# A hybrid decoder block on one core: the gated blocks exchanged inside SBUF, the left-side sums of down begun a group sooner, and a fourth pair by seven products

## The chip, the cores and the metric

The kernel runs on one NeuronCore of a Trainium2 chip. The metric is device time in microseconds of one execution; lower is better. The engines are named as in the profile: PE is TensorE's matmuls and PEld its weight loads, DVE is VectorE, ACT is ScalarE, POOL is GpSimd, SP is the engine that here only issues DMAs. L12 is line 12 of the kernel's source.

## The reference

One layer of a decoder block on 256 tokens of width 2048, everything in float32. The change lies in the two feed-forward halves (FFN 1 and FFN 2):

```
def swiglu(x, w_gu, w_down):
    gate, up = jnp.split(x @ w_gu, 2, axis=-1)      # 2048 -> 2 x 5632
    return (jax.nn.silu(gate) * up) @ w_down        # 5632 -> 2048

h = h + 0.5 * swiglu(rms_norm(h, ffn1_norm), ffn1_w_gu, ffn1_w_down)
h = h + hybrid_mixer(rms_norm(h, mix_norm), ...)    # gated DeltaNet and stick-breaking heads
h = h + 0.5 * swiglu(rms_norm(h, ffn2_norm), ffn2_w_gu, ffn2_w_down)
h = h + sigmoid(rms_norm(h, ple_norm) @ ple_w_gate) * (p @ ple_w_proj)
return rms_norm(h, final_norm)
```

## The kernel before

**Float32 out of two halves.** Every float32 operand is split into a rounded high half and the rest (`whi` and `wlo` for weights, `hTh` and `hTl` for activations), and each product is three matmuls: high by high, low weight by high, high weight by low. A weight pair (256 rows by 512 columns) is loaded into `raw` (SP's queue, four buffers), cast to `whi` by ACT (L77) and reduced to `wlo` by DVE (L78), two pairs ahead of its use. It then feeds 12 matmuls of 128x128 by 512 columns.

**Groups.** An FFN runs in three parts of 3, 4 and 4 blocks of 512 hidden columns (`PARTS`). Each part has its gate/up groups ("gu", one for each block: banks g0, g1, u0, u1) and then two down groups ("dn", two output blocks of 512 each, all in banks named d). A group has some of its pairs by seven products instead of eight (Strassen's scheme over two token halves and two column halves), and the others plainly. The number by products is `NS` = 4 for gate/up; for down, `NS_DOWN` gives 2 in part 0 and 3 in parts 1 and 2.

**Products.** A product needs a weight sum and a left-side sum. The weight quarters `R` (1 MB for four pairs) come on POOL's queue; their sums are formed by DVE (L307) or by accumulating DMAs; each of the seven is cast to `shi` by ACT (L298) and reduced to `slo` by DVE (L299), two buffers each, and feeds 3 matmuls per pair (L342 to L344). The seven products of a group are computed in the middle of the group ahead of it, between that group's plain pairs. The left-side sums (`halves`, L423: `S`, then its halves `Sh` and `Sl`) are made from the activations' halves: `S` by DVE (L455, L461), `Sh` by ACT (L463), `Sl` by DVE (L464). For down they begin with the last gate/up group of a part (L525).

**From up to down.** When a gate/up group's gate is done, ACT applies Silu (`gated`, L508). When up is done, `down_input` (L473) multiplies (`sil`, L480), transposes in blocks of 32 by 32 (`tb`, L485), exchanges the blocks through DRAM (four writes `scr`, L491, then one read `tT`, L496) and splits the result into `hTh` (L502) and `hTl` (L503), which the plain down matmuls and the left-side sums read. The writes go out on ACT's queue, and on SP's for the last block of a part.

**What sets the order.** `plan` writes one list of weight pairs, sums and loads, which is followed as it stands. Side work lives in generators on `lanes` (lane 0: the exchange; lane 1: left-side sums): each plain pair advances every lane by one step, `finish` runs a lane out, and a `yield` is one step's delay. A scheduler then orders each engine's instructions by its own costs; `keep_in_program_order` pins one. Each DMA also takes one of eight semaphores in turn, and waits until the earlier transfer on that semaphore has landed.

Of the kernel before, what the change touches and what calls it, by code (L numbers as in the profile page):

```python
# [20 lines left out]
NB = 512  # L21
# [5 lines left out]
PARTS = ((0, 3), (3, 7), (7, 11))  # L27


NS = 4  # L30
NS_DOWN = tuple(3 if i1 - i0 == 4 else 2 for i0, i1 in PARTS)


SEVEN = (0, 1, 2, 4, 3, 5, 6)
# [12 lines left out]
def block_kernel(ctx, tc, a, out):  # L47
    nc = tc.nc
# [4 lines left out]
    act = ctx.enter_context(tc.tile_pool(name="act", bufs=1))  # L53
# [9 lines left out]
    lanes = Lanes(4)  # L63
    dr = ctx.enter_context(tc.tile_pool(name="dr", bufs=1, space=bass.MemoryType.DRAM))
# [358 lines left out]
    def halves(kind, his, los, ns, wait=0):  # L423


        for _ in range(wait):
            yield
        fp = current[0]

        sh = fp.tile([P, NS, 2, 2, P], F32R, tag="Sh", name="Sh")  # L430
        sl = fp.tile([P, NS, 2, 2, P], F32R, tag="Sl", name="Sl")

        def side(i, g):
            if i in (0, 4, 6):
                k, t = 2 * (g % 2) + (i > 0), i // 6
                c = slice(t * P, (t + 1) * P)
                return his[g // 2][:, k, c], los[g // 2][:, k, c]
            j, t = {1: (1, 1), 2: (0, 0), 3: (0, 1), 5: (1, 0)}[i]
            return sh[:, g, j, t, :], sl[:, g, j, t, :]

        sides[kind] = side

        for g0 in range(0, ns, 2):
            n = min(2, ns - g0)
            hi, lo = his[g0 // 2], los[g0 // 2]
            keep = lambda ins: ins
            if g0 and n == 1:

                keep = tc.keep_in_program_order
                yield  # L450
            if n == 2:
                x = fp.tile([P, 2 * NB], F32, tag="sil", name="S")
            else:
                x = act.tile([P, NB], F32, tag="nat", name="S", bufs=4)
            keep(nc.vector.tensor_tensor(out=x, in0=hi[:, 0:2 * n].bitcast(F32).rearrange("p k x -> p (k x)"),  # L455
                                         in1=lo[:, 0:2 * n].bitcast(F32).rearrange("p k x -> p (k x)"), op=ALU.add))
# [7 lines left out]
            nc.vector.tensor_tensor(out=sx[1], in0=x, in1=sx[0], op=ALU.subtract)  # L464
            yield

    def ffn(n, nT, r, scale, next_norm, stat):
        xs = picker(*nT)
        late = callable(r)
        with tc.tile_pool(name="ffn", bufs=1) as fp:  # L470
            hTh, hTl = [], []

            def down_input(u, sil, th, tl, last):  # L473

                queue, keep = (nc.sync, lambda x: x) if last else (nc.scalar, tc.keep_in_program_order)
                for t in range(2):
                    nc.vector.scalar_tensor_tensor(out=sil[:, t, :], in0=u[t], scalar=r[:, t:t + 1], in1=sil[:, t, :],  # L480
                                                   op0=ALU.mult, op1=ALU.mult)
                yield
                tb = fp.tile([P, 4, 2, P], F32, tag="tT", name="tb")
                for t in range(2):
                    nc.vector.transpose(tb[:, :, t].rearrange("p c (j x) -> p c j x", j=4),  # L485
                                        sil[:, t, :].rearrange("p (j c x) -> p c j x", j=4, c=4))
                if not last:
                    yield
                scr = dr.tile([P, 4, 2, P], F32, tag="scr2", name="scr2", bufs=2)
                for q in range(4):  # L490
                    keep(queue.dma_start(out=scr[:, q].rearrange("(c x) t i -> x c (t i)", c=4),  # L491
                                         in_=tb[32 * q:32 * q + 32].rearrange("x c t i -> x c (t i)")))
                for _ in range(2 if last else 4):
                    yield
                tT = fp.tile([P, 4, 2, P], F32, tag="tT", name="tT")
                keep(nc.sync.dma_start(out=tT, in_=scr))  # L496
                for _ in range(last or 6):
                    yield
                for t in range(2):
                    hi, lo = (x[:, :, t * P:(t + 1) * P].rearrange("p j (q y) -> p q j y", q=4) for x in (th, tl))  # L500
                    tv = tT[:, :, t].rearrange("p q (j y) -> p q j y", j=4)
                    keep(nc.scalar.copy(hi, tv))  # L502
# [8 lines left out]
            nxt = None  # L511
            current[0] = fp
            lanes.add(1, halves("gu", *nT, NS, 6 if late else 0))
            for group, todo in ffn_plan[n]:
                if group.kind == "behind":
                    break
                dn = group.kind == "dn"
                i0 = PARTS[group.part][0]

                if dn and group.nb and not group.last:  # L520
                    lanes.add(1, halves("gu", *nT, NS))
                elif dn and group.nb and group.follower:
                    lanes.add(1, halves("behind", *nxt, NS_BEHIND, 4))
                elif not dn and group.follower.kind == "dn":
                    lanes.add(1, halves("dn", hTh[i0:], hTl[i0:], NS_DOWN[group.part]))  # L525
                if dn and group.last and nxt is None:
                    nxt = new_nT()
                if group.banks is None:
                    group.new_banks()
                for kind, one in todo:  # L530
                    if kind == "seventh":
                        group.follower.product(SEVEN[one])
                        continue
                    b, g = one
                    whi, wlo = next_weights()
                    for j in range(2):
# [3 lines left out]
                        for t in range(2):  # L540
# [3 lines left out]
                            nc.tensor.matmul(out, xh[:, c], wlo[:, j, :], start=False, stop=False, skip_group_check=True)  # L544
                            nc.tensor.matmul(out, xl[:, c], whi[:, j, :], start=False, stop=sp, skip_group_check=True)  # L545
                    lanes.step()
                    if g < len(group.src[b]) - 1:
                        continue
                    outs = group.banks[2 * b:2 * b + 2]
                    if dn:  # L550
                        nb = group.nb + b
                        for t in range(2):
                            hb = h[:, t, block(nb)]
                            nc.vector.scalar_tensor_tensor(out=hb, in0=outs[t], scalar=scale, in1=hb,
                                                           op0=ALU.mult, op1=ALU.add)
                            if group.last:
                                sumsq(stat, t, block(nb), nb)
                        if group.last:
                            norm_block(nxt, next_norm, nb, lambda: fp.tile([P, 2, 4, P], F32, tag="tT", name="tT"),
                                       mm_ps if group.follower or n == "2" else mx_ps)  # L560
                            lanes.advance(0)
                    elif b == 0:
                        if not late:
                            sil = gated(outs)
                    else:
                        if late:
                            r = r()
                            sil = gated(group.banks[0:2])
                            late = False
# [12 lines left out]
                        if last:  # L582
                            lanes.advance(0)
# [797 lines left out]
```

## Time and profile before

| | |
|---|---|
| median of 3 runs | 1948.04 us (1947.73 to 1949.59) |
| profiled execution | 1948.68 us |
| its span | 1947.0 us |
| granted TensorE clock | 0.999 of full speed |
| PE busy | 1930.5 us, 99% |
| PEld busy | 1593.0 us, 82% |
| DVE busy | 1569.3 us, 81% |
| ACT busy | 1163.5 us, 60% |
| DMA | 475.04 MB, 244 GB/s on average |

The span runs from the first to the last instruction; the execution's own time has 1.68 us around it. Matmuls overlap, so that PE's busy share says little: what counts is how far apart the starts of matmuls lie, and where they lie further apart than in an undisturbed stream. A row of waits has the engine, the line, what it waited for, the total in us, the times and the longest. A row of a window has the stretch, then busy us and the number of instructions of PE, PEld, DVE, ACT and POOL, the clock, the DMA share and GB/s.

### The profile page before, as it was taken

How to read it: one execution, taken by the hardware profiler on the slowest of the kernel's cores; microseconds unless marked ns; L12 is line 12 of the kernel's file. 1: busy time of each engine (PE TensorE's matmuls, PEld its weight loads, DVE VectorE, ACT ScalarE, POOL GpSimd, SP SyncE). 2: the span in 40 equal slices, each digit the busy share in tenths (PEclk: the TensorE clock that was granted, in tenths of full speed). 3: DMA queues.
4: the chain of work that ended last, by engine and by line, in shares of the span. 5: the costliest groups of instructions: out<-in, count | busy, mean ns of one | idle time of the engine just before them, and what ended most of it. 6: DMA issues, size and time to landing. Idle time of an engine off the chain costs nothing.

```text
span 1947.0 us, 24130 instructions
## 1 busy us (share of the span) xinstructions
PE 1930.5 (99%) x8884; PEld 1593.0 (82%) x8884; DVE 1569.3 (81%) x1679; ACT 1163.5 (60%) x1358; POOL 148.4 (8%) x226
## 2 busy tenths in 40 slices
PE   9999999999999999999999999999999999999998
PEld 8888888888888888878788888888888888888886
DVE  7889878997889766797856579899888987888865
ACT  7656666566565557664555456566565755656654
POOL 0011100000010000010100000010000100001000
PEclk9999999999999999999999999999999999999999
DMA  8778888788887765556565786788898987888764
GB/s 314 267 238 282 254 296 273 229 294 250 279 284 240 225 219 170 176 171 208 171 204 160 242 290 227 225 291 283 243 281 249 314 260 240 272 255 293 232 213 144
DMA packets 144182, 475.04 MB, mean 244 GB/s; under 512 B 19649, under 2 KB 47297, under 8 KB 129857
## 3 DMA queue, kind: packets, MB, share of 16 engines
q1 hardware_dynamic: 107200, 302.16, 43.9%
q0 software_dynamic: 25920, 160.44, 30.2%
q10 hardware_dynamic: 10944, 10.91, 1.8%
q8 instruction: 69, 1.13, 0.2%
q14 instruction: 49, 0.39, 0.1%
HBM read 451.44 MB, written 22.02 MB: 243 GB/s over the span
## 4 chain that ended last, share of the span: by engine, by line
PE 88%; DVE 7%; DMA 3%; ACT 1%; issue 1%; POOL 0%; SPq 0%; POOLq 0%; DVEq 0%; ACTq 0%
PE d L545 5%; PE d L543 5%; PE d L544 5%; PE g L343 4%; PE g L344 4%; PE g L342 4%; PE u L544 4%; PE u L545 4%; PE u L543 4%; PE g L544 4%; PE g L545 4%; PE pj L112 4%; PE pj L113 4%; PE pj L114 4%; PE g L543 4%; PE d L343 2%
## 5 line engine op out<-in xcount | busy, mean ns | idle before, releaser
L77 ACT CAST whi<-raw 128x1024 fp32r<-128x1024 f32 (+1 forms) x489 | 512.1, 1050 | 422.7 <-PE pj L114 99.0
L78 DVE TENSOR_TENSOR wlo<-raw,whi 128x1024 fp32r<-128x1024 f32 (+1 forms) x489 | 592.3, 1218 | 162.3 <-ACT whi L77 161.2
L299 DVE TENSOR_TENSOR slo<-R,shi 128x2048 fp32r<-128x2048 f32 (+2 forms) x224 | 444.9, 1989 | 140.0 <-ACT shi L298 138.2
L298 ACT CAST shi<-R 128x2048 fp32r<-128x2048 f32 (+2 forms) x224 | 373.5, 1671 | 128.5 <-DVE R L307 62.7
L112 PE MATMUL pj<-whi,nTh 128*128 128x512 f32 x448 | 179.4, 401 | 0.0
L113 PE MATMUL pj<-wlo,nTh 128*128 128x512 f32 x448 | 175.2, 391 | 1.1 <-DVE wlo L78 1.1
L114 PE MATMUL pj<-whi,nTl 128*128 128x512 f32 x448 | 174.9, 390 | 0.0
L543 PE MATMUL d<-whi,hTh 128*128 128x512 f32 x448 | 174.5, 390 | 0.0
L544 PE MATMUL d<-wlo,hTh 128*128 128x512 f32 x448 | 174.3, 389 | 0.0
L545 PE MATMUL d<-whi,hTl 128*128 128x512 f32 x448 | 173.4, 389 | 0.0
L544 PE MATMUL g<-wlo,nTh 128*128 128x512 f32 x400 | 156.0, 390 | 0.5 <-DVE wlo L78 0.5
L544 PE MATMUL u<-wlo,nTh 128*128 128x512 f32 x400 | 155.7, 389 | 0.4 <-DVE wlo L78 0.4
L545 PE MATMUL g<-whi,nTl 128*128 128x512 f32 x400 | 155.8, 389 | 0.0
L545 PE MATMUL u<-whi,nTl 128*128 128x512 f32 x400 | 155.7, 389 | 0.0
L543 PE MATMUL g<-whi,nTh 128*128 128x512 f32 x400 | 155.3, 390 | 0.0
L543 PE MATMUL u<-whi,nTh 128*128 128x512 f32 x400 | 154.1, 389 | 0.0
L307 DVE TENSOR_TENSOR R<-R 128x2048 f32<-128x2048 f32 (+2 forms) x68 | 135.8, 1996 | 0.1
L113 PEld LDWEIGHTS pj<-wlo,nTh 128*128 128x128 f32 x448 | 84.2, 188 | 18.9 <-DVE wlo L78 2.6
L543 PEld LDWEIGHTS d<-whi,hTh 128*128 128x128 f32 x448 | 84.1, 188 | 18.2 <-ACT hTh L502 1.0
L545 PEld LDWEIGHTS d<-whi,hTl 128*128 128x128 f32 x448 | 84.1, 188 | 17.8
L114 PEld LDWEIGHTS pj<-whi,nTl 128*128 128x128 f32 x448 | 84.1, 188 | 17.5
L544 PEld LDWEIGHTS d<-wlo,hTh 128*128 128x128 f32 x448 | 84.1, 188 | 17.4
(332 smaller groups left out, 3444.1 us busy)
## 6 DMA issues: line engine op xcount, KB each, us to landing
raw<-in_w_gu SPq DMA_DIRECT2D x199, 512.0 KB, 5.7
raw<-in_w_down SPq DMA_DIRECT2D x112, 512.0 KB, 6.9
raw<-in_w_in SPq DMA_DIRECT2D x112, 512.0 KB, 3.4
R<-in_w_gu2q POOLq DMA_DIRECT2D x54, 1024.0 KB, 8.6
R<-in_w_gu1q POOLq DMA_DIRECT2D x48, 1024.0 KB, 8.6
raw<-in_w_out SPq DMA_DIRECT2D x32, 512.0 KB, 4.5
tT<-scr SPq DMA_DIRECT2D x22, 512.0 KB, 5.0
R<-in_w_down11q POOLq DMA_DIRECT2D x12, 768.0 KB, 6.2
```

The lines of the kernel that those rows point to most:

```text
L77: nc.scalar.copy(hi[:, j, :], raw[:, j, :])
L78: nc.vector.tensor_tensor(out=lo[:, j, :], in0=raw[:, j, :], in1=hi[:, j, :], op=ALU.subtract)
L112: nc.tensor.matmul(outs[t], xh[:, c], whi[:, j, :], start=st, stop=False)
L113: nc.tensor.matmul(outs[t], xh[:, c], wlo[:, j, :], start=False, stop=False)
L114: nc.tensor.matmul(outs[t], xl[:, c], whi[:, j, :], start=False, stop=sp)
L298: keep(nc.scalar.copy(hi, w))
L299: nc.vector.tensor_tensor(out=lo, in0=w, in1=hi, op=ALU.subtract)
L307: keep(nc.vector.tensor_tensor(out=self.raw[x], in0=self.raw[x], in1=self.raw[y], op=ALU.add))
L343: nc.tensor.matmul(out, xh, wlo[:, g, :], start=False, stop=False, skip_group_check=True)
L543: nc.tensor.matmul(out, xh[:, c], whi[:, j, :], start=st, stop=False, skip_group_check=True)
L544: nc.tensor.matmul(out, xh[:, c], wlo[:, j, :], start=False, stop=False, skip_group_check=True)
L545: nc.tensor.matmul(out, xl[:, c], whi[:, j, :], start=False, stop=sp, skip_group_check=True)
```

## The change

It has four pieces. `NS_DOWN` goes from (2, 3, 3) to (2, 4, 3): in part 1's two down groups, which have eight pairs a side, four pairs go by products instead of three. The exchange goes from SBUF to SBUF: 16 transfers of 32 partitions by 1 KB, all on SP's queue, take the place of four writes and one read; the tiles `S` and `tT` swap their buffers. The left-side sums of down begin at the sixth product that is computed in the group before the last gate/up group, and what is left of older sums on that lane is run out there. And Silu is issued two plain pairs later.

```
-NS_DOWN = tuple(3 if i1 - i0 == 4 else 2 for i0, i1 in PARTS)
+NS_DOWN = (2, 4, 3)
...
@@ halves
-            if g0 and n == 1:
-                keep = tc.keep_in_program_order
-                yield
-            if n == 2:
-                x = fp.tile([P, 2 * NB], F32, tag="sil", name="S")
-            else:
-                x = act.tile([P, NB], F32, tag="nat", name="S", bufs=4)
+            x = fp.tile([P, 2 * NB], F32, tag="tT", name="S")[:, 0:n * NB]
...
@@ down_input
-                if not last:
+                for _ in range(0 if last else 3):
                     yield
-                scr = dr.tile([P, 4, 2, P], F32, tag="scr2", name="scr2", bufs=2)
+                tT = fp.tile([P, 4, 2, P], F32, tag="sil", name="tT")
                 for q in range(4):
-                    keep(queue.dma_start(out=scr[:, q].rearrange("(c x) t i -> x c (t i)", c=4),
-                                         in_=tb[32 * q:32 * q + 32].rearrange("x c t i -> x c (t i)")))
-                for _ in range(2 if last else 4):
-                    yield
-                tT = fp.tile([P, 4, 2, P], F32, tag="tT", name="tT")
-                keep(nc.sync.dma_start(out=tT, in_=scr))
-                for _ in range(last or 6):
+                    for c in range(4):
+                        keep(nc.sync.dma_start(out=tT[32 * c:32 * c + 32, q], in_=tb[32 * q:32 * q + 32, c]))
+                for _ in range(last or 2):
                     yield
...
@@ ffn
-                elif not dn and group.follower.kind == "dn":
-                    lanes.add(1, halves("dn", hTh[i0:], hTl[i0:], NS_DOWN[group.part]))
...
                     if kind == "seventh":
-                        group.follower.product(SEVEN[one])
+                        follower = group.follower
+                        follower.product(SEVEN[one])
+                        if not dn and one == 5 and follower.kind == "gu" and follower.follower.kind == "dn":
+                            lanes.finish(1)
+                            lanes.add(1, halves("dn", hTh[i0:], hTl[i0:], NS_DOWN[group.part]))
+                            lanes.advance(1)
                         continue
...
                     lanes.step()
+                    if waiting:
+                        waiting -= 1
+                        if not waiting:
+                            sil = gated(group.banks[0:2])
...
                     elif b == 0:
-                        if not late:
+                        if group.ns:
+                            waiting = 2
+                        elif not late:
                             sil = gated(outs)
...
-                        last = (3 if i1 - i0 == 4 else 2) if len(hTh) == i1 else 0
+                        last = (5 if NS_DOWN[group.part] == 3 else 4) if len(hTh) == i1 else 0
```

In the changed source the exchange is L484, the sums `S`, `Sh`, `Sl` are L447 to L456, the splits L490 and L491, the multiplication and the transposes L472 and L477, the plain matmuls L534 to L536.

**SP, at the first exchange of FFN 1** (`raw` are weight loads; before's four writes are on ACT's queue). Before:

```order
L74 DMA raw_580<-in_w_gu10 128x1024
L74 DMA raw_598<-in_w_gu10 128x1024
L74 DMA raw_616<-in_w_gu10 128x1024
L74 DMA raw_634<-in_w_gu10 128x1024
L496 DMA tT_652<-scr2_575 128x1024
L74 DMA raw_654<-in_w_gu10 128x1024
```

Now:

```order
L74 DMA raw_575<-in_w_gu10 128x1024
L74 DMA raw_593<-in_w_gu10 128x1024
L484 DMA tT_611<-tb_546 32x256 x16
L74 DMA raw_628<-in_w_gu10 128x1024
L74 DMA raw_646<-in_w_gu10 128x1024
L74 DMA raw_668<-in_w_gu10 128x1024
```

The sixteen transfers stand ahead of two weight loads that went before the one read.

**DVE, in front of part 1's first down group, FFN 1** (`slo` are the splits of down's weight sums, `wlo` those of plain pairs). Before:

```order
L464 TENSOR_TENSOR Sl_2725<-S_2726,Sh_2724 128x1024
L455 TENSOR_TENSOR S_2780<-hTh_2382,hTl_2383 128x512
L299 TENSOR_TENSOR slo_2803<-R_2548,shi_2802 128x1536
L461 TENSOR_TENSOR S_2780<-S_2780 128x128
L78 TENSOR_TENSOR wlo_2809<-raw_2807,whi_2808 128x1024
L461 TENSOR_TENSOR S_2780<-S_2780 128x128
L78 TENSOR_TENSOR wlo_2844<-raw_2842,whi_2843 128x1024
L461 TENSOR_TENSOR S_2780<-S_2780 128x128
L78 TENSOR_TENSOR wlo_2880<-raw_2878,whi_2879 128x1024
L461 TENSOR_TENSOR S_2780<-S_2780 128x128
L78 TENSOR_TENSOR wlo_2945<-raw_2943,whi_2944 128x1024
L464 TENSOR_TENSOR Sl_2725<-S_2780,Sh_2724 128x512
```

Now:

```order
L299 TENSOR_TENSOR slo_2760<-R_2597,shi_2759 128x2048
L453 TENSOR_TENSOR S_2741<-S_2741 128x2x128
L307 TENSOR_TENSOR R_2597<-R_2597,R_2633 128x2048
L453 TENSOR_TENSOR S_2741<-S_2741 128x2x128
L78 TENSOR_TENSOR wlo_2794<-raw_2792,whi_2793 128x1024
L78 TENSOR_TENSOR wlo_2817<-raw_2815,whi_2816 128x1024
L456 TENSOR_TENSOR Sl_2720<-S_2741,Sh_2719 128x1024
L299 TENSOR_TENSOR slo_2799<-R_2597,shi_2798 128x2048
L477 STREAM_TRANSPOSE tb_2789<-sil_2657 128x4x128 x2
L307 TENSOR_TENSOR R_2597<-R_2597,R_2679 128x2048
L78 TENSOR_TENSOR wlo_2857<-raw_2855,whi_2856 128x1024
L78 TENSOR_TENSOR wlo_2909<-raw_2907,whi_2908 128x1024
```

The last `Sl` stood behind the second split and four weight splits; now it stands ahead of the second split, and the splits are 2048 wide instead of 1536.

**DVE, at the end of that group's products** (`sil` the multiplication by up of the part's last block, `tb` its transposes). Before:

```order
L299 TENSOR_TENSOR slo_2936<-R_2548,shi_2935 128x1536
L480 SCALAR_TENSOR_TENSOR sil_2825<-u1_2454,rstd2_515,sil_2825 128x512
L503 TENSOR_TENSOR hTl_2678<-tT_2896,hTh_2677 128x4x4x32 x2
L299 TENSOR_TENSOR slo_2995<-R_2876,shi_2994 128x1536
L485 STREAM_TRANSPOSE tb_2977<-sil_2825 128x4x128 x2
```

Now:

```order
L472 SCALAR_TENSOR_TENSOR sil_2968<-u0_2488,rstd2_515,sil_2968 128x512
L299 TENSOR_TENSOR slo_3015<-R_2597,shi_3014 128x2048
L472 SCALAR_TENSOR_TENSOR sil_2968<-u1_2489,rstd2_515,sil_2968 128x512
L477 STREAM_TRANSPOSE tb_3052<-sil_2968 128x4x128 x2
L78 TENSOR_TENSOR wlo_3092<-raw_3090,whi_3091 128x1024
```

The transposes moved ahead of the next group's first split.

More of the change, by code (lines that the diff above doesn't have):

```diff
@@ L445, in halves @@
             hi, lo = his[g0 // 2], los[g0 // 2]
-            keep = lambda ins: ins
-            if g0 and n == 1:
-                keep = tc.keep_in_program_order
-                yield
-            if n == 2:
-                x = fp.tile([P, 2 * NB], F32, tag="sil", name="S")
-            else:
-                x = act.tile([P, NB], F32, tag="nat", name="S", bufs=4)
-            keep(nc.vector.tensor_tensor(out=x, in0=hi[:, 0:2 * n].bitcast(F32).rearrange("p k x -> p (k x)"),
-                                         in1=lo[:, 0:2 * n].bitcast(F32).rearrange("p k x -> p (k x)"), op=ALU.add))
+            x = fp.tile([P, 2 * NB], F32, tag="tT", name="S")[:, 0:n * NB]
+            nc.vector.tensor_tensor(out=x, in0=hi[:, 0:2 * n].bitcast(F32).rearrange("p k x -> p (k x)"),
+                                    in1=lo[:, 0:2 * n].bitcast(F32).rearrange("p k x -> p (k x)"), op=ALU.add)
             xv = x.rearrange("p (g j t y) -> p g j t y", g=n, j=2, t=2)
@@ L473, in down_input @@
             def down_input(u, sil, th, tl, last):
-                queue, keep = (nc.sync, lambda x: x) if last else (nc.scalar, tc.keep_in_program_order)
+                keep = (lambda x: x) if last else tc.keep_in_program_order
                 for t in range(2):
@@ L509, in gated @@
                 return sil
-            nxt = None
+            nxt, waiting = None, 0
             current[0] = fp
```

## The prediction, made before the changed kernel ran

> **What bounds the kernel now.** I read the page first, then the matmuls in order of time, then what the matmuls and their weight loads waited for, the busy times by stretches of 10 us, and the chain around the places where the matmuls thin out.
>
> ```profile
> span 1947.0 us, 24130 instructions
> PE 1930.5 (99%) x8884; PEld 1593.0 (82%) x8884; DVE 1569.3 (81%) x1679; ACT 1163.5 (60%) x1358; POOL 148.4 (8%) x226
> 357.30 0.39 PE L343 MATMUL d<-slo,Sh 128*128 128x512 f32 x1
> 357.53 0.39 PE L344 MATMUL d<-shi,Sl 128*128 128x512 f32 x1
> ```
>
> TensorE is busy 99% of the span: the chain that ends last is its stream of matmuls. The last two rows set the price of a matmul: each lasts 0.39 us, but its neighbour begins 0.23 us later, since they overlap. Over long undisturbed stretches I read 0.2268 us from start to start. So a matmul that is left out is worth 0.227 us, not 0.39.
>
> ```profile
> PEld d L343 <- DVE slo L299: 4.8, 8, 0.6
> 350.00:360.00 10.00, 10.00 (x45) 8.27 (x45) 9.86 (x14) 6.95 (x8) 0.88 (x1) 1.00 0.74 225
> 360.00:370.00 10.00, 9.86 (x43) 7.44 (x41) 5.72 (x7) 6.65 (x8) 0.56 (x1) 1.00 0.81 270
> 370.00:380.00 10.00, 9.78 (x43) 7.81 (x42) 9.65 (x10) 6.61 (x7) 1.63 (x3) 1.00 0.90 320
> 610.00:620.00 10.00, 9.87 (x43) 7.46 (x42) 7.25 (x7) 7.85 (x11) 1.12 (x2) 1.00 0.78 286
> 620.00:630.00 10.00, 9.78 (x44) 7.75 (x43) 9.64 (x11) 5.48 (x6) 1.07 (x2) 1.00 0.85 305
> 1510.00:1520.00 10.00, 9.86 (x43) 7.73 (x42) 8.13 (x8) 9.73 (x11) 1.62 (x3) 1.00 0.78 286
> 1520.00:1530.00 10.00, 9.78 (x43) 7.77 (x43) 10.00 (x10) 4.99 (x5) 1.40 (x2) 1.00 0.75 258
> 1760.00:1770.00 10.00, 9.64 (x41) 7.35 (x40) 9.65 (x10) 8.36 (x9) 1.95 (x4) 1.00 0.76 272
> ```
>
> The row of waits (total us, times, longest) is the largest of its kind and still small: the weight loads of down's products wait for `slo`, the low half of a weight sum, eight times. The windows (busy us and count of PE, then PEld, DVE, ACT, POOL, then clock, DMA share, GB/s) show them: an undisturbed 10 us touches 45 or 46 matmuls, while those at 360-380, 610-630, 1510-1530 and 1760-1770 touch 43, 43; 43, 44; 43, 43; and 41. Two or three starts lost per window, times 0.227, is 1.0 to 1.2 us at each of the four, and adding up all start-to-start gaps over 0.227 gives 1.19, 1.22, 1.19 and 0.96: 4.56 us. These are the entries into down: 360 and 1510 in part 1 (the second part), 610 and 1760 in part 2. The granted clock is 1.00 throughout.
>
> ```profile
> 363.59 0.68 DVE L464 TENSOR_TENSOR Sl<-S,Sh 128x512 fp32r<-128x512 f32 x1
> 365.62 1.27 ACT shi L298
> 366.92 0.55 DVE slo L299
> 375.37 1.77 DVE slo L299
> 376.57 0.39 PE L342 MATMUL d<-shi,hTh 128*128 128x512 f32 x1
> 377.18 0.50 PE L343 MATMUL d<-slo,hTh 128*128 128x512 f32 x1 [0.22 <-DVE slo L299]
> 611.25 0.69 DVE L464 TENSOR_TENSOR Sl<-S,Sh 128x512 fp32r<-128x512 f32 x1
> 614.58 1.76 DVE L299 TENSOR_TENSOR slo<-R,shi 128x1536 fp32r<-128x1536 f32 x1 [2.65 <-ACT shi L298]
> ```
>
> The cause in this trace: the left-side sums finish at 364.27. The product that reads them can't finish before, so its `shi` buffer (there are two) stays taken until then; the next `shi` starts at 365.62, its `slo` at 366.92, and five splits must then run back to back while VectorE also has stt, transposes and weight splits. The last comes just too late: 0.61 us between the matmuls at 376.57 and 377.18. In part 2 the same chain stands at 611.25 and 614.58.
>
> **The change, part by part.**
>
> ```profile
> L299 DVE TENSOR_TENSOR slo<-R,shi 128x2048 fp32r<-128x2048 f32 x133 | 304.4, 2290 | 111.7 <-ACT shi L298 111.3
> L299 DVE TENSOR_TENSOR slo<-R,shi 128x1536 fp32r<-128x1536 f32 x56 | 98.0, 1756 | 19.2 <-ACT shi L298 18.6
> L307 DVE TENSOR_TENSOR R<-R 128x2048 f32<-128x2048 f32 x42 | 95.7, 2280 | 0.1
> L307 DVE TENSOR_TENSOR R<-R 128x1536 f32<-128x1536 f32 x16 | 27.9, 1747 | 0.0
> L77 ACT CAST whi<-raw 128x1024 fp32r<-128x1024 f32 (+1 forms) x489 | 512.1, 1050 | 422.7 <-PE pj L114 99.0
> L78 DVE TENSOR_TENSOR wlo<-raw,whi 128x1024 fp32r<-128x1024 f32 x487 | 590.9, 1220 | 161.3 <-ACT whi L77 160.2
> ```
>
> *Four pairs by seven products* in part 1's two down groups, in both FFNs: four groups. A pair column costs 24 matmuls plainly and 21 by products, so 3 fewer per group, 12 in all: -12 x 0.2268 = -2.72 us. VectorE pays per group 7 x (2.290 - 1.756) + 2 x (2.280 - 1.747) - 2 x 1.220 = +2.37 us, 9.5 us in all; ScalarE's casts grow by less. It costs nothing where VectorE has room: 8 plain pairs and 7 products of 12 matmuls make 15 x 2.72 = 40.8 us of TensorE, and the VectorE work of the first down group with the second's splits is 8 x 1.220 + 7 x 2.290 + 2 x 2.280 = 30.4, with the small subtractions and the exchange some 35 us. The next stretch (second down group, gate/up's splits) has gate/up's left-side sums on top, 2 x 4.1, in all 41.7 us: no room, where before it was 44.1 in 46.2. The buffers carry that overhang, or it costs up to 0.9 us per FFN.
>
> *Sums begun a group sooner.* The work is the same, apart from the fourth pair's share (1.22 + 4 x 0.42 + 1.22 against 0.69 + 4 x 0.29 + 0.69: 1.6 us of VectorE per FFN). By the order, all of part 2's sums but the last pair's tail stand before the down products' first split, so the product no longer holds its `shi` buffer. I take both part-2 stalls as gone: -(1.22 + 0.96) = -2.18, ends 0 (the bunching stays) and -2.18. In part 1 the same holds for the sums, but each split is 0.53 us longer, and the third product's `slo` now stands behind stt, sums and two transposes. Bounds: all gone, -1.19 each; or more stall by the fifth split's overhang, +1.0 each. I take 0.3 us less each, -0.6, nearest to what before shows there, since seven splits of 0.53 us more use up 3.7 us of the earlier start.
>
> *The gate by two steps later* (Silu) moves two short ScalarE instructions per group behind weight casts. up's stt, which reads it, comes seven pairs, over 19 us, later: nothing.
>
> *The exchange.*
>
> ```profile
> SPq L74 <- DVE wlo L78: 1218.2, 384, 9.8
> raw<-in_w_gu SPq DMA_DIRECT2D x199, 512.0 KB, 5.7
> scr<-tb ACTq DMA_DIRECT2D x64, 128.0 KB, 5.3
> tT<-scr SPq DMA_DIRECT2D x22, 512.0 KB, 5.0
> sc<-dec SPq DMA_DIRECT2D x8, 32.0 KB, 2.4
> L1069 SPq DMA_DIRECT2D Z<-sc x8: 325/442/449, 866.0 to 943.2; - x8
> ```
>
> Each of 22 exchanges was two hops, 5.3 + 5.0 us landing; now it is one hop of 16 transfers of 32 KB. The nearest rows have 0.44 us to issue one and 2.4 us to land. Issue: 16 x 0.44 = 7.0 us; by the order each transfer also waits for the eighth before it. So one exchange takes 7.0 + 2.4 = 9.4 us, or, with the landing of a loaded queue, 7.0 + 5.3 = 12.3, during which SP issues no weights. Against it SP stands idle 1218 us for free weight buffers. In a group with products a weight load comes every 40.8 / 8 = 5.1 us; four buffers give 20.4 us from a load to its use, of which landing 5.7, cast 1.05 and split 1.22 take 8.0: 12.4 us of room. Even 12.3 fits: nothing. What waits behind SP is weight loads alone; product quarters are on POOL's queue. 64 issues leave ScalarE's queue, which had room.
>
> The Trainium skill, DMA: Bandwidth & Descriptors, Rules for kernel authors, speaks against this: small transfers should be merged, for under 64 KB one pays mostly overhead. Its fit (Anatomy of one DMA, 2.0 us + bytes / 436 GB/s, given for POOL's path) makes an estimate of 2.08 us for 32 KB; the trace's 2.4 agrees. By the page 7.0 + 2.1 = 9.1 us stand in place of 9.4: no other sum.
>
> *The last exchange of part 1* has less cover: by the order its values are wanted 100 matmuls after the last of up, 22.7 us, where before it was 155, 35.2 us.
>
> ```profile
> 368.20 0.40 PE L545 MATMUL u<-whi,nTl 128*128 128x512 f32 x1
> 380.57 1.30 DVE L485 STREAM_TRANSPOSE tb<-sil 128x512 f32<-128x512 f32 x2
> 395.03 1.14 ACT L502 CAST hTh<-tT 128x512 fp32r<-128x512 f32 x2 [0.87 <-DMA tT<-scr]
> ```
>
> Before, the transposes ended at 381.87, 13.7 us after up's last matmul (368.20), and the exchange took 13.2. Now they stand directly behind the seventh split, some 7 us after up, plus 9.4 to 12.3: 16.4 to 19.3 of 22.7. It fits with 3 us to spare: nothing.
>
> *The first exchange* has no such room: it lies in a plain group, where four buffers are 4 x 2.72 = 10.9 us, less 8.0: 2.9 us.
>
> ```profile
> 50.82 10.56 SPq L74 DMA_DIRECT2D raw<-in_w_gu  x4
> 66.11 1.46 SPq L74 DMA_DIRECT2D raw<-in_w_gu  x2
> scr<-tb ACTq DMA_DIRECT2D x4, 128.0 KB, 7.8
> 65.00 0.50 PE L343 MATMUL u<-slo,Sh 128*128 128x512 f32 x1 [0.34 <-DVE slo L299]
> ```
>
> SP waited there anyway: after four loads that took until 61.4 the next went at 66.11. The landing of the exchange's writes in this stretch (the third row) was 7.8 us. By the order the exchange starts after two of the four loads between 50.82 and 61.4 and displaces two. Before, the gaps between matmuls over 60-80 add up to 1.1 us above 0.227 each, one of them at 65.00. The ends: no change, and +2 us (one issue of 7.0 over the room of 2.9, less half for what the order moves ahead). I take +0.6, nearer the row of before.
>
> Sum: -2.72 - 2.18 - 0.6 + 0.6 = -4.9, and +0.5 for the over-full second stretch (0.25 per FFN, between nothing and its 0.9): -4.4. The profiled execution took 1948.68, which is 0.64 above the median 1948.04 (1947.73 to 1949.59); against the median 1948.04 - 4.4 = **1943.6 us**. What this kernel's measurement can tell from no change I set at 0.2%, 3.9 us: below 1944.1 is faster, above 1951.9 slower.
>
> **The rivals.**
> - *All four entries cured*: splits start so early that part 1 doesn't stall either. -2.72 - 4.56 = -7.3, startup unchanged: 1940.8. For it: the cause is one and the same. Against: longer splits.
> - *Only the matmuls are saved*: the splits are still bunched behind VectorE's other work, and the stalls stay. -2.7: 1945.3. For it: VectorE was 9.65 and 10.00 of 10 us busy right behind the entries.
> - *VectorE takes it back*: the 9.5 + 3.2 us more VectorE work comes out on TensorE in part 1, where the second window is over-full, by 0.9 us per FFN and 1.0 at each entry, over the sum with part 2's stalls gone: -4.4 + 0.6 + 3.3 = -0.5: 1947.5.
> - *Slower: the first exchange starves the weights*. SP holds 7.0 us of issues and a landing of 7.8, 14.8 us, where 2.9 are covered: up to +11.9 in place of my 0.6, thus -5.0 + 11.9 = +6.9: 1954.9. It decides against the change from 8.9 us lost there. Against it: SP waited for buffers in the same stretch, and two loads go ahead. The Trainium skill's rule on small transfers, if each paid its overhead one after the other, would give 16 x 2.08 = 33 us for an exchange; the order lets eight be under way.
>
> **How the numbers follow.** My sum 0.40, all cured 0.19, only the matmuls 0.18, taken back 0.12, slower 0.11. My sum's own terms reach from 1942 to 1946, and 0.7 of it is below 1944.1; all cured is; of the rest a tenth is: 0.28 + 0.19 + 0.03 = 0.50 faster. Slower 0.10, the same 0.40. For 8 in 10 the range takes in all four lower cases with 1 us on the low end for the stalls that I can't place, and on the high end half of the last case's way: 1939.8 to 1950.5.
>
> **What would show it.** Right: 12 fewer matmuls; at 612-630 and 1755-1770 of before's clock windows of 45 again; the wait of `d` L343's weight loads for `slo` under 2.5 us (4.8 before); SP's waits for `wlo` down by about the 22 x 7 us of issue; no wait of matmuls for `wlo` above before's outside the startup. Wrong: thin windows at each exchange, or whi casts waiting for raw loads (weights late); full-busy VectorE with matmuls waiting for `slo` or `Sl` in part 1; a gap of several us at 60-80.

## The result, and the profile after

The changed kernel takes **2014.78 us** (median of 4 runs, 2010.18 to 2017.0), the kernel before 1948.72 (1947.73 to 1949.59): ratio 1.0336, 95% interval 1.0317 to 1.0355. It is 66 us slower, and lies outside the predicted range. The first lines of its page, its line on the exchange's transfers among the DMA issues, and the row of the line that issues them (duration min/median/max in ns):

```profile
span 2015.3 us, 24438 instructions
PE 1951.2 (97%) x8872; PEld 1602.1 (79%) x8872; DVE 1582.8 (79%) x1671; ACT 1167.4 (58%) x1350; POOL 148.4 (7%) x226
PE 59%; DVE 14%; DMA 11%; SPq 6%; issue 6%; ACT 4%; POOL 0%; DVEq 0%; ACTq 0%; POOLq 0%
...
tT<-tb SPq DMA_DIRECT2D x352, 32.0 KB, 3.7
L484 SPq DMA_DIRECT2D tT<-tb x352: 507/590/2323, 55.9 to 1846.6; - x176
```

Twelve matmuls fewer, as foreseen. But the chain that ended last, which was TensorE's stream, now has SP's issues, DMA landings, DVE and ACT in it. By the first matmuls of each phase, both FFNs lost 34.4 us each, the mixer nothing, and the tail gained 0.8. Four windows show where, in the columns explained ahead of the prediction:

```profile
330.00:340.00 10.00, 6.74 (x25) 5.21 (x24) 7.04 (x9) 4.18 (x5) 0.55 (x1) 0.82 0.77 291
410.00:420.00 10.00, 5.59 (x23) 4.03 (x23) 5.51 (x6) 7.14 (x7) 0.08 (x1) 0.92 0.71 234
420.00:430.00 10.00, 10.00 (x34) 8.00 (x34) 7.57 (x6) 3.46 (x4) 1.36 (x2) 0.74 0.86 222
670.00:680.00 10.00, 8.71 (x25) 6.71 (x25) 7.94 (x6) 6.14 (x7) 0.88 (x1) 0.66 0.80 206
```

Where 45 matmuls stood there are now 23 to 34, and the granted clock falls to 0.66. The place at 333 in SP's issues, and in the chain, each row with its start, its length and what it was:

```profile
303.91 7.18 SPq L74 DMA_DIRECT2D raw<-in_w_gu  x2
314.19 13.26 SPq L484 DMA_DIRECT2D tT<-tb  x16
327.54 16.15 SPq L74 DMA_DIRECT2D raw<-in_w_gu  x6
```

```profile
310.77 8.63 DMA raw<-in_w_gu
319.42 1.11 SPq L484
...
326.32 6.33 DMA tT<-tb
...
332.96 1.23 DVE S L447
...
335.12 2.21 DVE slo L299
...
337.38 0.79 PE g L343
338.18 0.43 PE g L344
338.60 0.43 PE g L342
```

One exchange holds SP for 13.26 us. Its eighth transfer waits some 0.9 us for a weight load that shares its semaphore and takes 8.63 us; its last lands at 332.65, 18.5 us after the first was issued (over the 22 exchanges the median is 16.0). DVE stands in front of `S`, the left-side sum that was moved sooner and that reuses the buffer from which the exchange still reads; behind it in DVE's line stands the `slo` for which TensorE waits 3.3 us. Then the matmuls start 0.43 us apart instead of 0.23. In the two FFNs 70 of these slow spacings were recorded, some 14 us; the rest of the lost time is waits. At the same place ACT stands as well, for the first weight load that SP could issue behind the exchange (at 327.54), and behind its cast stand the split `hTh` and the next `shi`:

```profile
333.73 1.05 ACT L77 CAST whi<-raw 128x1024 fp32r<-128x1024 f32 x1 [5.56 <-DMA raw<-in_w_gu]
334.68 1.13 ACT L490 CAST hTh<-tT 128x512 fp32r<-128x512 f32 x2
335.72 1.89 ACT L298 CAST shi<-R 128x2048 fp32r<-128x2048 f32 x1
```

Over the whole kernel, who stood in line for DMAs, and what reached TensorE:

```profile
ACT whi L77 <- DMA raw<-in_w_gu: 63.9, 19, 6.5
ACT hTh L490 <- DMA tT<-tb: 35.0, 7, 7.2
DVE S L447 <- DMA tT<-tb: 17.9, 4, 6.8
DVE S L447 <- DMA raw<-in_w_gu: 13.0, 2, 6.7
ACT whi L77 <- DMA raw<-in_w_down: 10.9, 8, 3.0
ACT hTh L490 <- DMA raw<-in_w_down: 10.4, 2, 5.9
PE d L343 <- DVE slo L299: 17.7, 13, 2.1
PE g L343 <- DVE slo L299: 13.0, 5, 3.3
PE d L342 <- ACT shi L298: 11.4, 6, 3.0
```

ACT and DVE stood 151 us for weights and exchanges (the first six rows; in two of them the releaser named is a weight load, though `S` and `hTh` come behind the exchange). The ACT wait for gate/up's `raw` was 3.2 us in the kernel before: weights now come late. They are issued late; once issued, a gate/up load landed in 6.2 us in the median, where it took 5.7 before.

### The profile page after: what moved, and what is told of

Same layout as the page of the kernel before. It is cut to its first block, busy times and chain, and to the rows that moved or that the text cites. A ratio compares the mean times of both kernels' runs of the same rounds, so it can differ in the third digit from the quotient of the medians.

```text
span 2015.3 us, 24438 instructions
## 1 busy us (share of the span) xinstructions
PE 1951.2 (97%) x8872; PEld 1602.1 (79%) x8872; DVE 1582.8 (79%) x1671; ACT 1167.4 (58%) x1350; POOL 148.4 (7%) x226
## 4 chain that ended last, share of the span: by engine, by line
PE 59%; DVE 14%; DMA 11%; SPq 6%; issue 6%; ACT 4%; POOL 0%; DVEq 0%; ACTq 0%; POOLq 0%
SPq L484 6%; DMA raw<-in_w_gu 6%; PE pj L112 4%; PE pj L113 4%; PE pj L114 4%; DVE wlo L78 3%; DVE slo L299 3%; PE d L535 3%; PE d L536 3%; PE d L534 3%; PE g L343 3%; PE g L344 3%; PE g L342 3%; DMA tT<-tb 3%; DMA raw<-in_w_down 2%
## 5 line engine op out<-in xcount | busy, mean ns | idle before, releaser
L77 ACT CAST whi<-raw 128x1024 fp32r<-128x1024 f32 (+1 forms) x481 | 503.9, 1050 | 469.4 <-PE pj L114 105.8
L78 DVE TENSOR_TENSOR wlo<-raw,whi 128x1024 fp32r<-128x1024 f32 (+1 forms) x481 | 583.0, 1217 | 204.2 <-ACT whi L77 202.8
L299 DVE TENSOR_TENSOR slo<-R,shi 128x2048 fp32r<-128x2048 f32 (+2 forms) x224 | 459.5, 2054 | 89.5 <-ACT shi L298 88.3
L298 ACT CAST shi<-R 128x2048 fp32r<-128x2048 f32 (+2 forms) x224 | 386.1, 1724 | 110.4 <-DVE R L307 71.3
L536 PE MATMUL d<-whi,hTl 128*128 128x512 f32 x416 | 163.0, 392 | 2.2 <-DVE hTl L491 2.2
L535 PE MATMUL d<-wlo,hTh 128*128 128x512 f32 x416 | 162.8, 391 | 0.0
L534 PE MATMUL d<-whi,hTh 128*128 128x512 f32 x416 | 162.3, 390 | 0.0
L534 PE MATMUL g<-whi,nTh 128*128 128x512 f32 x400 | 155.0, 390 | 1.1 <-ACT whi L77 0.9
L536 PE MATMUL g<-whi,nTl 128*128 128x512 f32 x400 | 155.9, 390 | 0.0
L536 PE MATMUL u<-whi,nTl 128*128 128x512 f32 x400 | 155.7, 389 | 0.0
L534 PE MATMUL u<-whi,nTh 128*128 128x512 f32 x400 | 155.6, 390 | 0.0
L112 PEld LDWEIGHTS pj<-whi,nTh 128*128 128x128 f32 x448 | 84.2, 188 | 16.7
L536 PEld LDWEIGHTS d<-whi,hTl 128*128 128x128 f32 x416 | 78.6, 189 | 20.4 <-DVE hTl L491 3.9
L343 PE MATMUL g<-slo,nTh 128*128 128x512 f32 x234 | 91.4, 391 | 0.7 <-DVE slo L299 0.7
```

Source lines behind the costliest of these rows:

```text
L77: nc.scalar.copy(hi[:, j, :], raw[:, j, :])
L78: nc.vector.tensor_tensor(out=lo[:, j, :], in0=raw[:, j, :], in1=hi[:, j, :], op=ALU.subtract)
L112: nc.tensor.matmul(outs[t], xh[:, c], whi[:, j, :], start=st, stop=False)
L298: keep(nc.scalar.copy(hi, w))
L299: nc.vector.tensor_tensor(out=lo, in0=w, in1=hi, op=ALU.subtract)
L343: nc.tensor.matmul(out, xh, wlo[:, g, :], start=False, stop=False, skip_group_check=True)
```

## The experiments

Times are medians; each ratio is to the kernel before on the same chip, with its 95% interval. The kernels were run on several chips, on which the kernel before took 1948.3 to 1948.9.

**One piece at a time.** Theories: A, the exchange itself (SP is held, weights come late, and ACT and DVE stand in line for its landing); B, the longer splits of four pairs; C, `S` waits for the exchange's buffer. From *own buffers for S* on, A is the hold of SP and the late weights alone, and the standing in line for the landing is theory D.

*The exchange alone* (`NS_DOWN`, the sums' start and Silu as before; `down_input` and the buffers of `S` as changed).

> The kernel before with the new exchange alone: 16 transfers inside SBUF on SP, tT and S in swapped buffers, the fewer steps ahead of the splits; three pairs, the sums begun in the last gate/up group and the early Silu stay. Theory A (the exchange carries the loss: SP is held 13 us at each of 22 exchanges, and DVE and ACT stand in line behind its landing): 2000 to 2015 us. Theory B (the loss is the four-pair products, whose longer splits come late): 1948 to 1953. Theory C (each piece is harmless, the loss comes from the earlier sums S waiting for the buffer that the exchange still reads): 1950 to 1965.

Measured: 2029.53 us, 1.0423 [1.0402, 1.0443]. That is above A's range too: the exchange carries the loss, and more than all of it, 81 us.

*All but the exchange.*

```
-                for q in range(4):
-                    for c in range(4):
-                        keep(nc.sync.dma_start(out=tT[32 * c:32 * c + 32, q], in_=tb[32 * q:32 * q + 32, c]))
+                for q in range(4):
+                    keep(queue.dma_start(out=scr[:, q]..., in_=tb[32 * q:32 * q + 32]...))
...
+                keep(nc.sync.dma_start(out=tT, in_=scr))
```

> The changed kernel with the old exchange through DRAM (and its steps); four pairs in part 1, the earlier sums and the later Silu stay. S of down is made for one pair at a time in another buffer, since the buffers of before don't allow the order; in part 0 of FFN 2, where the slow exchange isn't done in time, the sums begin as before. Theory A: 1941 to 1946, the forecast of the prediction without its startup term. Theory B: 1975 or more. Theory C: 1941 to 1950.

Measured: 1951.73, 1.0017 [1.0007, 1.0027]. Theory B falls as the cause of the loss, though the time is above A's and C's ranges too. But the three pieces did not gain with the old exchange either.

*Four pairs alone*, `NS_DOWN = (2, 4, 3)` in the kernel before.

> The kernel before with four pairs by seven products in part 1's down groups alone (the third and fourth pair's S each in a small buffer, the last exchange's splits one step sooner). Theories A and C: -2.7 us of matmuls against some more stall at the entries of part 1, 1945 to 1952. Theory B: 1975 or more, with matmuls of down waiting for slo in part 1 for over 15 us.

Measured: 1959.24, 1.0053 [1.0038, 1.0068]: above A's and C's 1952, far below B's 1975. With the sums still late, the 2048-wide splits and the sums together keep DVE from `wlo`: up's matmuls waited 4.6 us for it, in 3 places.

*The earlier sums alone.*

> The kernel before with down's sums begun a group sooner alone (S for one pair at a time; part 0 of FFN 2 as before). The prediction's step: the entry stalls of parts 1 and 2 go, -2.2 to -4.6 us, 1943.5 to 1946. Theory C without its cause, the new exchange: the same. If the stalls at the entries don't come from the late sums: 1947 to 1949.

Measured: 1954.52, 1.0030 [1.0018, 1.0042], a miss for every case. TensorE's waits there:

```profile
PE d L343 <- DVE slo L299: 4.1, 6, 1.3
PE u L546 <- DVE wlo L78: 3.5, 5, 0.8
```

The sums now stand ahead of weight splits of the last gate/up group, and the entries still stall. (Making `S` by single pairs costs VectorE a little too: it was busy 3 us longer.)

*Silu two steps later alone*, and *Silu and the earlier sums together*, both with the old exchange.

> The kernel before with Silu two steps later alone. The prediction's step: nothing, 1947 to 1950. If it orders ACT better ahead of the entries: 1943 to 1946.

> The kernel before with the earlier sums and the later Silu, three pairs in part 1, the old exchange. The earlier sums alone took 5.6 us more, with waits of up's matmuls for wlo just ahead of the entries (3.5 us in all), and all three pieces together 2.8 more. If the later Silu is what takes these waits away: 1945 to 1948. If not: 1953 to 1956.

Measured: 1949.44, 1.0002 [0.9993, 1.0011], nothing, as the prediction had it; and 1953.62, 1.0025 [1.0016, 1.0034]: Silu's place is not what was missing.

**Which part of the exchange.** First the two waits that the trace showed.

*Own buffers for S*: each pair's `S` in a 2 KB buffer of its own.

> The changed kernel with down's sums S made a pair at a time in the small buffers, so that no S waits for the buffer from which the exchange still reads (in the trace of after DVE waited 17.9 us in 4 places for the exchange there, in front of the splits of down's products). Theory A (SP is held 10 to 14 us by the issues of each exchange, so that weights come late): 2000 to 2015, hardly less. Theory C (DVE's wait for that buffer): 1955 to 1980, and the 3 us stalls in front of the last gate/up groups gone.

Measured: 2027.81, 1.0415 [1.0389, 1.0442], above A's range and far from C's. DVE's wait went (4.5 us left), and the time rose by 13 us. A new wait is part of it: made one pair at a time the sums take more of the lane's steps, which would make them late. The changed kernel has no wait of down's products for `Sh`; here it is:

```profile
PE d L342 <- ACT Sh L459: 17.7, 4, 7.5
```

Even without these 17.7 us the time would be some 2010, so C falls as the cause; some 5 us of it may be hidden here.

*Nobody waits for the landing*: as own buffers for S, but the splits read the blocks ahead of the exchange, so that down gets its input in the wrong places.

```
-                    tv = tT[:, :, t].rearrange("p q (j y) -> p q j y", j=4)
+                    tv = tb[:, :, t].rearrange("p q (j y) -> p q j y", j=4)
```

> The kernel of the run before in this list, with all 16 transfers issued and landing as they do, but the splits hTh and hTl read the transposed blocks ahead of the exchange (so down's input is in the wrong places): no instruction waits for the exchange's landing but those that reuse its buffers. Theory A (SP's issues): within 10 us of the kernel before it in the list. Theory D (ACT and DVE stand in line for the landing, 35 us of ACT in after): 1945 to 1965.

Measured: 2026.11, 1.0397 [1.0380, 1.0413], as A had it; but the trace shows that something waited after all. In these two kernels, the first row is of own buffers, the second of nobody waits:

```profile
ACT whi L77 <- DMA raw<-in_w_gu: 96.4, 21, 10.8
```

```profile
ACT sil L500 <- DMA tT<-tb: 104.7, 15, 9.7
```

With the readers gone, ACT stood for Silu's result buffer, which is the one the exchange writes. ACT's wait for weights went down from 103 to 19.5 us (gate/up and down) at the same time: one wait took the other's place.

*Eight transfers of sixteen*, the same otherwise (`for c in range(q % 2, 4, 2)`).

> As the run before, with 8 of the 16 transfers of each exchange left out, two of each of the four source blocks kept. Theory A: SP is held some 5 instead of 12 us, inside the room of the weight buffers, and the loss that the run before still has falls by more than half. Theory D: the same time as the run before, within 3 us.

Measured: **1942.12**, 0.9970 [0.9957, 0.9982]. All of the loss is gone with half of the transfers, as A had it and D not. But this does not part the two: the landing came sooner as well (the last transfer 7.0 us after the first in the median, instead of 16.0), and ACT no longer stood for Silu's buffer. SP at the exchange that began at 314 above:

```profile
307.42 5.81 SPq L488 DMA_DIRECT2D tT<-tb  x8
313.33 30.80 SPq L74 DMA_DIRECT2D raw<-in_w_gu  x8
```

*Two queues*: the changed kernel, every second transfer issued by ACT.

> The changed kernel with every second transfer issued by ACT instead of SP. Theory A: SP's hold falls to about half, weights come in time, and the exchange lands sooner: 1960 to 1985, unless ACT's 8 x 0.6 us per exchange in front of its casts takes the place, 2000 or more. Theory D: the landing comes some 4 us sooner, 1980 to 2000.

Measured: 2027.78, 1.0409 [1.0393, 1.0424]. That is A's second case, in which ACT's issues take the place, and far from D's. SP's hold fell to a median of 5.6 us, and the loss stayed. ACT's own work now stands behind transfers that wait for a semaphore (the first two rows), and `hTh` still for the landing (the third):

```profile
ACT shi L298 <- DMA tT<-tb: 22.0, 3, 8.9
ACT u L347 <- DMA tT<-tb: 20.8, 8, 3.7
ACT hTh L490 <- DMA tT<-tb: 19.7, 6, 6.1
```

The Trainium skill (DMA: Bandwidth & Descriptors, Issuing engines are not separate DMA queues) says that issuing from several engines saves the issuing time only; the trace agrees, and shows a price: ACT, which now issued half of them, stood in SP's place.

*Sixteen transfers into DRAM*: as nobody waits, with `tT` a DRAM tile.

> As the run in which nobody waits for the landing, but the 16 transfers write to DRAM instead of the buffer that Silu's result needs next (the splits again read the blocks ahead of the exchange, so down's input is in the wrong places): in that run ACT still stood 104.7 us in 15 places for that buffer. SP is held by 16 issues as before. Theory A (SP's hold, weights late): 2000 or more. Theory D (engines that stand in line for the landing, in whatever buffer): 1942 to 1955, that is no more than the run with half the transfers took, 1942, and a little for SP.

Measured: 1958.33, 1.0050 [1.0032, 1.0067], above D's range by 3 us and far below A's. It is not quite the same hold: into DRAM an issue took less (0.42 us in the median where inside SBUF it takes 0.59), and SP was held 9.2 us in the median instead of 12.1.

```profile
L488 SPq DMA_DIRECT2D scr<-tb x352: 302/420/1534, 55.9 to 1789.0; - x176
ACT whi L77 <- DMA raw<-in_w_gu: 47.2, 20, 6.4
```

*No transfers* and *twelve transfers* (all but those that stay in their quarter of the partitions), else as nobody waits.

> The run in which nobody waits without any transfer (the splits read the blocks ahead of the exchange, so down's input is in the wrong places): the other three pieces with an exchange that costs nothing. If the run with half the transfers (1942.1) was free of any loss: 1940 to 1943. The prediction's terms without the startup's 0.6 and with all entries cured: 1948.8 - 2.7 - 4.6 = 1941.5.

> The run in which nobody waits (2026.1 with sixteen transfers, 1942.1 with eight) with twelve transfers, those between different quarters of the partitions. If each transfer over eight costs the same: some 1984. If the loss sets in where the landing passes the place at which Silu wants the buffer: 1942 to 1960 with ACT's wait for it mostly gone, or, if it has passed, nearer to 2026.

Measured: 1942.04, 0.9965 [0.9952, 0.9979]; and 1965.12, 1.0085 [1.0070, 1.0100], which is in none of the ranges given for twelve. Eight transfers cost nothing (1942.12 against 1942.04), twelve cost 23 us, sixteen 84: no line, but a point between eight and twelve from which it rises ever more steeply in these counts. In the table, SP's hold is from the first issue to the end of the last, summed over the 22 exchanges; "stood" is ACT's and DVE's waits for the FFN's weight loads and the exchange's transfers.

| kernel | transfers | SP held, us | stood, us | time, us |
|---|---|---|---|---|
| no transfers | 0 | 0 | 4.9 | 1942.0 |
| half | 8 | 122 | 5.5 | 1942.1 |
| into DRAM | 16 | 208 | 50 | 1958.3 |
| twelve | 12 | 191 | 62 | 1965.1 |
| nobody waits | 16 | 268 | 128 | 2026.1 |
| own buffers for S | 16 | 268 | 134 | 2027.8 |
| the changed kernel | 16 | 266 | 151 | 2014.8 |

The hold alone does not order the times: into DRAM SP was held longer than with twelve transfers (208 us against 191), and yet less was stood (50 against 62) and lost. The changed kernel, the only one without own buffers for `S`, is out of line with the others.

*Begun sooner*: the transfers issued by the program three plain pairs sooner, the splits in place.

```
-                for _ in range(0 if last else 3):
+                for _ in range(0):
...
-                for _ in range(last or 2):
+                for _ in range(last or 5):
```

> The kernel with S in the small buffers (2027.8), all 16 transfers and all data in place, with the transfers of the blocks that are not a part's last issued three plain pairs (about 8 us) sooner; the splits stay where they are. Theory A (SP's hold): SP issues as much as before, 2015 to 2030. Theory D (readers in line for the landing): the wait of ACT for hTh's input and the Silu behind it go for 16 of 22 exchanges, 1960 to 1990; what is left is at the entries into down.

Measured: 2031.74, 1.0427 [1.0412, 1.0441]. It tells nothing of theory D, though its number is near A's: but for the first exchange of FFN 1, the scheduler left the transfers at the same places among SP's loads, so that they started no sooner.

**Versions.** *Five transfers through DRAM, at the new exchange's places and with its steps*, with own buffers for `S`.

```
+                scr = dr.tile([P, 4, 2, P], F32, tag="scr2", name="scr2", bufs=2)
                 for q in range(4):
-                    for c in range(4):
-                        keep(nc.sync.dma_start(out=tT[32 * c:32 * c + 32, q], in_=tb[32 * q:32 * q + 32, c]))
+                    keep(nc.sync.dma_start(out=scr[:, q].rearrange("(c x) t i -> x c (t i)", c=4),
+                                         in_=tb[32 * q:32 * q + 32].rearrange("x c t i -> x c (t i)")))
+                keep(nc.sync.dma_start(out=tT, in_=scr))
```

> The changed kernel with S in the small buffers and the exchange by five larger transfers through DRAM (four of 128 KB and one of 512 KB, all on SP), at the places and with the steps of the new exchange, and with all data where it belongs. Theories A and D agree that five transfers in two hops of some 5 us hold SP and the waiting engines for about half as long as sixteen: 1942 to 1950. If the count of transfers is not what matters but the wait for the landing, two hops are as long as before: 1960 to 2030.

Measured: 1954.49, 1.0033 [1.0020, 1.0046], some 5 us above what A and D allow. Most of the loss is gone; the rest stands in part 1's first down group.

*The same with three pairs.*

> The kernel with five transfers through DRAM (1954.5, with stalls of 2.4 to 2.9 us in part 1's first down group, where the last exchange comes late) with three pairs in part 1 as before the change, which gives that exchange some 12 us more cover: the stalls go, the matmuls come back, 1943 to 1947. If the stalls there are not from the last exchange: 1955 to 1958.

Measured: **1943.76**, 0.9976 [0.9965, 0.9986], 5.0 us faster than the kernel before and 71 faster than the changed one. The entries of part 1 and part 2 in FFN 1, and SP at the exchange that began at 314 above:

```profile
370.00:380.00 10.00, 10.00 (x46) 8.28 (x45) 8.98 (x10) 4.56 (x5) 0.54 (x1) 1.00 0.92 303
620.00:630.00 10.00, 10.00 (x46) 8.29 (x45) 9.53 (x10) 5.39 (x5) 1.43 (x2) 1.00 0.82 249
307.28 1.99 SPq L488 DMA_DIRECT2D scr<-tb  x4
310.59 1.49 SPq L74 DMA_DIRECT2D raw<-in_w_gu  x2
314.03 0.33 SPq L490 DMA_DIRECT2D tT<-scr  x1
```

SP issues two weight loads between the two hops, and TensorE's stream is whole. The Trainium skill (DMA: Bandwidth & Descriptors, Rules for kernel authors) asks for small transfers to be merged; these runs agree, for with four pairs and own buffers for `S` in both, two hops of five larger transfers (1954.49) beat one hop of sixteen small ones (2027.81) by 73 us.

*Five transfers in the kernel before, without the other pieces*, and *the faster version once more*.

> The kernel before with the exchange by five transfers through DRAM, all on SP, at the places and with the steps and buffers of the new exchange; three pairs, the sums in the last gate/up group and the early Silu stay. If the exchange's place and steps are the gain: 1943 to 1946. If it needs the earlier sums beside it, since then the stalls at the entries remain: 1947 to 1953.

> The version by five transfers through DRAM with three pairs, earlier sums and later Silu once more, beside the run above: 1942 to 1946, faster than the kernel before by 0.15 to 0.35%.

Measured: 1951.45, 1.0014 [1.0005, 1.0023]; and 1943.76 again, 0.9976 [0.9967, 0.9986]. The shorter exchange and the earlier sums gain only together: the sums alone cost 5.6 us, the five transfers alone 2.7, and both with the later Silu gain 5.0. Both without the later Silu, which alone did nothing, was not run.

## Why the prediction was wrong

- **The step that failed is "Even 12.3 fits: nothing".** SP's hold was 12.1 us in the median, inside the 9.4 to 12.3 given, but by luck: these were 7.0 of issues and a landing, while the sixteen issues took 11.0 (0.69 each on average, not 0.44), with some 0.9 between them, and the last landing came 16.0 us after the first issue. What was wrong above all was the room of 12.4 us, reckoned from a weight load to the matmuls that use it. The first customer of a late load is ACT, which casts in order and two pairs ahead. Behind 14 of the 22 exchanges the cast of the first weight loaded after it stood for 2.5 to 6.5 us; the hold less this wait, 5.6 to 9.5 us, is what there was of room (at 314: 13.26 - 5.56 = 7.7). Behind the waiting cast stand `hTh` and `shi`, and the products need `shi` at once. That no one else would wait, "What waits behind SP is weight loads alone", left out whom the weight loads hold up. The trace of the kernel before could have told: there a gate/up weight had landed 8.7 us, in the median, when its cast began. The prediction's own sign of being wrong, thin windows and `whi` casts that wait for `raw`, is what came.
- **The readers of the exchange were not costed.** The change cut the steps between the transfers and their readers; I took a hop as shorter and asked only of a part's last exchange when its values are wanted. In the trace the exchange at 314 took 18.5 us to its last landing, and ACT and DVE, in order, stood for it. That `S` moved into the buffer which the exchange reads stood in the diff; it was a wait added and not named.
- **The slower rival had the right engine and the wrong place.** It was priced at the first exchange only. There the gaps over 60-80 rose from 1.1 to 3.6 us, past the +2 that I gave as the end, and 0.9 of the 2.5 remain without any transfer; the other 60 us and more came in groups that I had said to have room.
- **The terms on matmuls and entries hold where the exchange is cheap.** With no transfers, and own buffers for `S`, the other pieces give 1942.0 against 1948.75, -6.7 us, close to the rival "all four entries cured", -7.3: part 2's stalls are gone, part 1's nearly, and a gap of 1.9 us is left at the startup. My likeliest case, with part 1's stalls kept and 0.5 for the over-full stretch, was too careful there. With the old exchange the same pieces gained nothing (1951.7), so these terms don't stand by themselves: I summed pieces that need each other.
- **VectorE did not take it back**: with half the transfers DVE carries all the added work, and the time is 1942.1.
- What stays open: how the changed kernel's loss divides between late weights and readers in line. Own buffers, no waiting readers and two queues each removed one wait and showed another in its place. That no engine stands in line for anything of the exchange while SP is held just as long was only approached (into DRAM: 9.2 us of hold, 16 us lost).

## What to carry to other kernels

Room for a late transfer is to be reckoned to the first instruction that waits in an in-order queue, not to the bound engine that uses its result in the end: list what stands behind that instruction. The trace of the kernel before has it, as the time from a landing to the first instruction that reads what landed. A cost that is hidden has a point from which it shows, so try it at half and at full size on the chip before believing in the room; here eight transfers were free and sixteen cost 84 us. When one wait is removed and the time stays, look in the same view for the wait that took its place.

## What was not expected of the hardware

- Issuing a transfer of 32 partitions by 1 KB took 0.59 us inside SBUF and 0.42 into DRAM (medians of 352 each), and up to 2.3 us; the long ones were mostly the last five of an exchange's sixteen. Spread over two queues an issue cost the same on both (0.59 on SP, 0.60 on ACT).
- After most waits of some 2 to 4 us in the changed kernel the matmuls started 0.43 us apart for up to 13 of them, and windows had a clock of 0.66 to 0.92. After two single waits, of 3.1 and 3.2 us at 1512 and 1775, they were back at about 0.23 after the first two, with the clock at 1.00, as it was with the stalls of 0.6 us in the kernel before. The Trainium skill (TensorE: Matmul & The Clock Gate, Wait — 56ns, not 53.3ns?) gives 426.7 ns from start to start for 512 columns while the array is cold; the trace agrees, with 0.43. By these spacings, a stall here cost up to an estimated 2.6 us (13 x 0.2) beyond its own length.
